# A two-layer hybrid mixer block: spare products redistributed around the triangular inverses, an ordering edge for the inverses' first matmuls, and the weights' low halves made in pieces of 256 columns

## The chip, the cores and the metric

The kernel runs on one core of one Trainium2 chip. The metric is the device time of one execution in microseconds (us). Three executions of the kernel before gave 1887.24, 1888.75 and 1889.05 us, so its median is 1888.75 us.

## The reference, cut to what matters

A block of depth 2 works on 512 tokens of width 1024 and on 256 context tokens. In each layer the normed and modulated activations `h` (and `hc` of the context) are projected by one wide matrix and split into three branches, their gates and three merge gates:

```python
parts = jnp.split(h @ w_in[layer], SPLIT_POINTS, axis=-1)
# a: gated delta rule, chunked, in both directions
lmat = jnp.where(strict, jnp.einsum('bhnid,bhnjd->bhnij', kb, k) * decay, 0.0)
tinv = lax.linalg.triangular_solve(lmat + eye, eye, left_side=True, lower=True)
# b: window attention with context keys; c: retention in both directions
merged = g_a * (y_a @ w_br[0]) + g_b * (y_b @ w_br[1]) + g_c * (y_c @ w_br[2])
x = x + gate * (merged @ w_o)
```

Branch a needs, per head, direction and chunk, the inverse of a unit triangular matrix. The gates of the three branches (`az`, `bz`, `cz`, four blocks of 128 columns each, through silu) and the merge gates (`m`, 24 blocks, through sigmoid) depend on `h` alone, not on what the branches compute. In layer 0 everything is also done for the context; in the last layer the context only needs what feeds keys and values.

## The kernel before, in words

Everything lies with channels on the partitions, 512 + 256 tokens along the free axis. A product with a block of 128 output columns (`proj`, line 317) splits the weights and the activations into a rounded high half and a low half: with eight blocks of 128 input channels it issues 16 matmuls with the high half of the weights (against `hh` and `hl`) and then 8 with the low half (`wl`, against `hh`), 24 of 512 columns into a PSUM bank of the pool `px` (two banks), and, where the context is wanted, 24 of 256 columns into the pool `pc` (one bank). `weight` (line 290) loads 512 KB by a DMA of the SP queue, makes the high half on ACT (line 278) and the low half on POOL by one subtraction of 128x1024 (line 287); `wr`, `wh` and `wl` have two buffers each. For the branch matrices of the merge there are four blocks of input channels, so half of all that.

**Spare products.** `aside` (line 1197) is a generator of 36 products a layer, in the order of `names`: az, bz, the first 8 of m, cz, and the other 16 of m. Each is read out of PSUM by ACT (tanh); an az, bz or cz also by one DVE instruction a bank (`stt`, line 281), which is the last reader of the bank. The result goes to DRAM by a DMA of the ACT queue and is loaded where it is needed. Since these products depend on `h` alone, the program mixes them into stages that are short of matmuls: `weave` interleaves generators, each with a number of steps, and `FILL` gives the number of spare products of each stage:

```python
weave((seq(self.delta_mats(l, last, st[0]), self.delta_inv(st[0])), 45),
      (self.delta_proj(l, 1, vec, last, st[1]), 6), fill(F[0]))
weave((self.hi(self.delta_chain(l, last, st[0])), 6), fill(F[1]))
weave((self.hi(self.delta_mats(l, last, st[1])), 4), fill(F[2]))
weave((self.hi(self.delta_inv(st[1])), 43), fill(F[3]))
weave((self.hi(self.delta_chain(l, last, st[1])), 6), fill(F[4]))
```

`F[5]` is the number after each of the attention's steps (12 in layer 0, 8 in layer 1) and `F[6]` the number before the token projection of branch c. What is left then is taken in the loop over `self.mods` and `self.fill` ahead of the merge. Before, layer 0 takes 20 in the five stages, 12 in the attention, 2 by `F[6]` and leaves 2; layer 1 takes 20, 8 and 2 and leaves 6.

**The inverses.** Heads go in two pairs, `st[0]` and `st[1]`. `delta_inv` (line 701) first inverts all 32x32 blocks on the diagonal at once by 31 steps of two DVE `tensor_tensor` each (lines 726 and 728, shown as line 284), each on the result of the last, with both inputs in SBUF. Then follow two transposes (731, 732) and 16 copies on DVE (747), with copies on ACT (749). `levels` (line 756) builds the 128x128 inverse from these by four bursts of small matmuls (line 774). A burst (line 262) chains its matmuls, so that they stand in one piece in TensorE's list, and makes the first of them wait for all that `made` names, the 16 DVE copies among it.

**What sets the order.** The framework writes each engine's list of instructions once, at compile time: at each moment of a modelled run it takes the ready instruction of the highest priority, where a place earlier in the program is a higher priority and `high_priority(offset)` raises it. On the chip each engine works through its list strictly in that order and waits at the head of it. The bursts, and in the second pair all of `delta_mats`, `delta_inv` and `delta_chain` (through `hi`), are raised by 3000; spare products and the projections have the plain priority and fill what is left. So a burst stands in TensorE's list at the place at which the modelled run had its inputs ready, with the spare products that weren't yet used up behind it.

After the second pair's chain come the normalisation of branch a, the attention, the token projection, the retention heads (`ret_head`), `c_norm` (line 936, ends in 16 to 24 `tensor_scalar` of line 954), the gates (`gated`, transposes of line 905), and the merge, whose first 8 products (branch a) don't depend on branch c.

Of the kernel before, what the change touches and what calls it, by code (L numbers as in the profile page):

```python
# [9 lines left out]
F32 = mybir.dt.float32  # L10
# [3 lines left out]
ALU = mybir.AluOpType  # L14
# [18 lines left out]
C1 = 3  # L33
AH = 2
BG = (0, 2)
FILL = ((2, 4, 2, 7, 5, 1, 2), (2, 3, 3, 7, 5, 1, 2))

NAMES = (["aq%d" % i for i in range(4)] + ["ak%d" % i for i in range(4)]
         + ["av%d" % i for i in range(4)] + ["az%d" % i for i in range(4)]
# [122 lines left out]
class Builder:  # L162
# [96 lines left out]
    def mm(self, out, lhsT, rhs, start=True, stop=True):  # L259
        return self.nc.tensor.matmul(out, lhsT=lhsT, rhs=rhs, start=start, stop=stop)  # L260

    def burst(self, todo, after):

        info = lambda c: mybir.DependencyInfo(c, mybir.DependencyReason.DATA)
        last = None
        with self.tc.high_priority(offset=HI):
            for f in todo:
                i = f().ins
                if last is None:
                    for a in after:  # L270
                        self.tc.add_manual_dep(i, a.ins.name, info(mybir.DependencyClass.Sync), reason="burst")
                else:
                    self.tc.add_manual_dep(i, last, info(mybir.DependencyClass.NoSync), reason="burst")
                last = i.name
# [15 lines left out]
    def weight(self, dram, kb=KB):  # L290
        nc = self.nc
        w = self.wr.tile([128, KB, 128], F32, name="wr")[:, 0:kb]
        hi = self.wh.tile([128, KB, 128], F32R, name="wh")[:, 0:kb]
        lo = self.wl.tile([128, KB, 128], F32R, name="wl")[:, 0:kb]
        with self.tc.high_priority(offset=WHI):
            nc.sync.dma_start(w, dram)
            self.act(hi, w, AF.Copy)
            self.gtt(lo, w, hi.bitcast(F32), ALU.subtract)
        return [hi[:, k] for k in range(kb)], [lo[:, k] for k in range(kb)]

    def prod(self, ps, w, acts, sl, ks=None):
        hi, lo = w
        n = len(acts)
        ks = ks or range(n)
        for k in ks:
            self.mm(ps, hi[k], acts[k][0].r[:, sl], start=(k == 0), stop=False)
            self.mm(ps, hi[k], acts[k][1].r[:, sl], start=False, stop=False)
        for k in ks:
            self.mm(ps, lo[k], acts[k][0].r[:, sl], start=False, stop=(k == n - 1))

    def proj(self, dram, acts, ctx, w=None):
        w = w or self.weight(dram, len(acts))
# [385 lines left out]
                self.free(df, db)  # L698
                yield

    def delta_inv(self, st):

        nc = self.nc
        Z, M, X = self.alloc_inv()
        nc.gpsimd.memset(Z, 0.0)
        nc.gpsimd.memset(X, 0.0)
        nc.gpsimd.memset(X[:, 0:1024:33], 1.0)
        blk = lambda s, q: s.f.rearrange("p (n c) -> p n c", c=128)[32 * q:32 * q + 32, :, 32 * q:32 * q + 32]  # L710
        sq = lambda t: t.rearrange("p (a b) -> p a b", b=32)
        lane = lambda t, q, d, hh: sq(t)[32 * q:32 * q + 32, :, d * 12 + hh * 6:d * 12 + hh * 6 + 6].rearrange(
            "p a n -> p n a")
        for hh, h in enumerate(st.heads):
            for q in range(4):
                self.act(lane(Z, q, 0, hh), blk(st.U[h], q), AF.Copy)
                nc.vector.transpose(out=lane(Z, q, 1, hh), in_=blk(st.U[h], q))
            yield
        nc.vector.transpose(out=M, in_=Z)
        yield  # L720
        mv, xv = sq(M), sq(X)
        ts = self.alloc()
        for m in range(31):
            n, w = 31 - m, m + 1
            tv = ts.f[:, 0:n * w].rearrange("p (r c) -> p r c", c=w)
            self.tt(tv, mv[:, m + 1:32, m:m + 1].to_broadcast([128, n, w]),
                    xv[:, m:m + 1, 0:w].to_broadcast([128, n, w]), ALU.mult)
            self.tt(xv[:, m + 1:32, 0:w], xv[:, m + 1:32, 0:w], tv, ALU.subtract)
            yield
        self.free(ts)  # L730
        nc.vector.transpose(out=Z, in_=X)
        nc.vector.transpose(out=sq(M), in_=xv.rearrange("p r c -> p c r"))
        yield
        W = st.W = {}
        T, Q = self.alloc(), self.alloc()
        nc.gpsimd.memset(Q.f, 0.0)
        six = lambda t: t.rearrange("p (h n c) -> p h n c", h=2, c=64)
        made = []
        for d in range(2):
            wsrc, tsrc = (Z, M) if d == 0 else (M, Z)  # L740

            own, other = (0, 2) if d == 0 else (3, 1)
            for hh, h in enumerate(st.heads):
                W[h, d] = self.alloc()
                nc.gpsimd.memset(W[h, d].f, 0.0)
                for q in range(4):
                    made.append(nc.vector.tensor_copy(blk(W[h, d], q), lane(wsrc, q, d, hh)))
                for q, t, c in ((own, Q, 32 * (own % 2)), (own + 1 - 2 * d, Q, 32 * (1 - own % 2)), (other, T, 0)):
                    made.append(self.act(six(t.f)[32 * q:32 * q + 32, hh, :, c:c + 32],
                                         lane(tsrc, q, d, hh), AF.Copy))  # L750
                yield
        self.free_inv()
        yield from self.levels(st, W, T, Q, made)
        self.free(T, Q, *st.U.values())

    def levels(self, st, W, T, Q, made):

# [8 lines left out]
        at = [(hh, h, ch) for hh, h in heads for ch in range(NCH)]  # L768
        sl = lambda a: slice(32 * a, 32 * a + 32)
# [3 lines left out]
        def mm(out, lhsT, rhs, pos):  # L773
# [2 lines left out]
        ps = bank(32)  # L776
        self.burst([mm(ps[sl(b), hh, ch], st.U[h].f[sl(a), ch * 128 + 32 * b:ch * 128 + 32 * b + 32],
                       t[sl(a), hh, ch, c:c + 32], (32 * a, 32 * b))
                    for hh, h, ch in at for a, b, d, t, c in pair], made)
        x = [self.act(xv[:, :, :, 0:32], ps, AF.Copy)]  # L780
        yield
        ps, pt = bank(32), bank(32)
# [414 lines left out]
    def aside(self, l, last):  # L1197
        nc = self.nc
        n = SEQ if last else TOK
        self.kept = {}  # L1200
        names = ["az%d" % i for i in range(4)] + ["bz%d" % i for i in range(4)]
        names += ["m%d_%d" % (r, d) for r in range(3) for d in range(8)]
        names[16:16] = ["cz%d" % i for i in range(4)]
        for nm in names:
            px, pc = self.pblk(l, nm, not last)
            t = self.fp.tile([128, TOK], F32, name="kept")
            for ps, sl in ((px, slice(0, SEQ)), (pc, slice(SEQ, TOK)))[:1 if last else 2]:
                self.act(t[:, sl], ps, AF.Tanh, scale=0.5)
# [15 lines left out]
    def layer(self, l, xs, rs, mod, vec, row, ada):  # L1224
# [9 lines left out]
        for k in range(KB):  # L1234
            self.tap("hh%d_%d" % (l, k), self.hs[k][0].f)
            self.tap("hl%d_%d" % (l, k), self.hs[k][1].f)
        self.fill = self.aside(l, last)
        self.mods = self.ada(ada) if ada else iter(())
        F = FILL[l]
# [37 lines left out]
        self.delta_gates(l, ba, row)  # L1277
        for _ in p0:
            pass
        weave((seq(self.delta_mats(l, last, st[0]), self.delta_inv(st[0])), 45),  # L1280
              (self.delta_proj(l, 1, vec, last, st[1]), 6), fill(F[0]))
        weave((self.hi(self.delta_chain(l, last, st[0])), 6), fill(F[1]))
        weave((self.hi(self.delta_mats(l, last, st[1])), 4), fill(F[2]))
        weave((self.hi(self.delta_inv(st[1])), 43), fill(F[3]))
        weave((self.hi(self.delta_chain(l, last, st[1])), 6), fill(F[4]))
        for t in st:
            oa.update(t.o)
# [154 lines left out]
def seq(*gens):  # L1442
    for g in gens:
        yield from g
# [34 lines left out]
```

## Time and profile before

| | |
|---|---|
| median of three executions | 1888.75 us |
| profiled execution | 1880.63 us |
| its span, first to last instruction | 1878.8 us |
| TensorE busy | 1721.2 us, 92% of the span |
| DVE, ACT, POOL busy | 1110.9, 844.3, 478.0 us |
| mean granted clock of TensorE | 0.968 of full speed |
| chain that ended last, by engine | PE 23%, DVE 7%, ACT 2% |

Where an engine is idle, the profile names the instruction whose end let it go on (its releaser). A line of the timeline merges like instructions that follow each other: start, time from first start to last end, engine, line, operation, output and inputs, count, and in brackets the idle time ahead of it with the releaser. The number behind a source line is that of the profile; helpers such as `mm` (260), `act` (278), `stt` (281), `tt` (284) and `gtt` (287) give their own line.

### The profile page before, as it was taken

To read this page: it belongs to the slowest core of one execution; us is meant where nothing else is said; L and a number is where in the kernel's file an instruction comes from. 1 tells how busy PE (TensorE), PEld (TensorE's weight loads), DVE (VectorE), ACT (ScalarE), POOL (GpSimd) and SP (SyncE) were. 2 spreads that over 40 slices of the span, in tenths; PEclk is the share of its full clock that TensorE was granted. 3 is DMA by queue.
4 is the path that set the end of the run, shared out by engine and by line. 5 is a ranking of instruction groups with operands and counts; after the bars stand their busy time and mean duration, and the time that the engine had idled before them with its cause. 6 is when DMAs were issued, how large, how long until landed. Compare 5 with 4: busy or idle time off the path is not lost. (4 is left out here: it accounts for less than half of the span.)

```text
span 1878.8 us, 30037 instructions
## 1 busy us (share of the span) xinstructions
PE 1721.2 (92%) x11574; PEld 1464.8 (78%) x11574; DVE 1110.9 (59%) x2531; ACT 844.3 (45%) x2018; POOL 478.0 (25%) x283
## 2 busy tenths in 40 slices
PE   7998799799899999999999899779698988999987
PEld 4887688698777779988888688668587766987876
DVE  4668948642663662355573648967856576253464
ACT  5564545442543553222223656456355465233234
POOL 1321402112212112122332513332213123123432
PEclk9999999899999999999999999889899999999998
DMA  8211112123234243115452111112223413114441
GB/s 309 69 35 42 65 30 92 64 94 120 83 108 155 85 135 112 43 51 169 130 176 96 63 41 67 51 62 68 94 76 119 140 62 113 34 57 160 152 153 68
DMA packets 73743, 180.63 MB, mean 96 GB/s; under 512 B 8832, under 2 KB 16384, under 8 KB 73600
## 3 DMA queue, kind: packets, MB, share of 16 engines
q1 hardware_dynamic: 62144, 154.07, 24.8%
q10 hardware_dynamic: 11456, 24.65, 3.4%
q8 instruction: 91, 1.49, 0.3%
q14 instruction: 52, 0.43, 0.1%
HBM read 150.89 MB, written 27.79 MB: 95 GB/s over the span
## 5 line engine op out<-in xcount | busy, mean ns | idle before, releaser
L287 POOL TENSOR_TENSOR wl<-wr,wh 128x1024 fp32r<-128x1024 f32 (+1 forms) x184 | 391.5, 2128 | 1215.7 <-ACT wh L278 811.6
L260 PE MATMUL px<-hh,wh 128*128 128x512 f32 (+1 forms) x1088 | 433.5, 402 | 22.8 <-DVE t L281 11.3
L260 PE MATMUL px<-hl,wh 128*128 128x512 f32 (+1 forms) x1088 | 432.2, 400 | 3.0 <-DVE hl L281 2.3
L284 DVE TENSOR_TENSOR t<-t,t 128x512 f32<-128x512 f32 (+21 forms) x411 | 299.0, 729 | 37.1 <-ACT t L278 25.6
L260 PE MATMUL px<-hh,wl 128*128 128x512 f32 (+1 forms) x1088 | 293.0, 400 | 0.0
L278 ACT ACTIVATE wh<-wr 128x1024 fp32r<-128x1024 f32 (+1 forms) x184 | 174.2, 947 | 213.8 <-PE pc L260 90.4
L260 PEld LDWEIGHTS px<-hh,wh 128*128 128x128 f32 x1088 | 209.6, 193 | 66.1 <-issue 10.7
L278 ACT ACTIVATE t<-t 32x192 f32<-32x192 f32 (+10 forms) x314 | 167.3, 545 | 207.0 <-DVE t L281 126.7
L260 PE MATMUL pg<-t,t 128*128 128x128 f32 (+2 forms) x1616 | 232.2, 287 | 21.0 <-DVE t L284 18.8
L260 PEld LDWEIGHTS px<-hl,wh 128*128 128x128 f32 x1088 | 210.1, 193 | 41.2 <-DVE hl L281 5.1
L260 PEld LDWEIGHTS pg<-t,t 128*128 128x128 f32 x1616 | 207.2, 192 | 43.7 <-issue 17.2
L260 PEld LDWEIGHTS px<-hh,wl 128*128 128x128 f32 x1088 | 202.6, 194 | 38.9 <-issue 2.0
L260 PE MATMUL pc<-hh,wh 128*128 128x256 f32 x696 | 177.6, 290 | 8.4 <-DVE t L281 7.8
L260 PE MATMUL pc<-hl,wh 128*128 128x256 f32 x696 | 179.0, 291 | 2.0 <-DVE hl L281 2.0
L260 PEld LDWEIGHTS pc<-hh,wh 128*128 128x128 f32 x696 | 134.8, 194 | 15.2 <-issue 7.1
L260 PEld LDWEIGHTS pc<-hl,wh 128*128 128x128 f32 x696 | 135.3, 194 | 7.3 <-DVE hl L281 3.2
L278 ACT ACTIVATE t<-pg 128x128 f32<-128x128 f32 (+4 forms) x216 | 77.6, 383 | 133.3 <-PE pg L403 37.1
L260 PE MATMUL pc<-hh,wl 128*128 128x256 f32 x696 | 103.7, 288 | 0.0
L278 ACT ACTIVATE t<-px 128x128 f32<-128x128 f32 (+2 forms) x120 | 54.4, 465 | 102.4 <-PE px L260 95.3
L260 PE MATMUL px<-t,wh 128*128 128x512 f32 x384 | 95.8, 392 | 0.1
L260 PEld LDWEIGHTS pc<-hh,wl 128*128 128x128 f32 x696 | 92.5, 195 | 0.8 <-issue 0.8
L260 PE MATMUL px<-t,hh 128*128 128x272 f32 (+1 forms) x384 | 88.3, 317 | 0.8 <-POOL t L287 0.6
(191 smaller groups left out, 2340.0 us busy)
## 6 DMA issues: line engine op xcount, KB each, us to landing
wr<-wblk SPq DMA_DIRECT2D x120, 512.0 KB, 3.2
t<-wada SPq DMA_DIRECT2D x48, 384.0 KB, 4.7
wr<-wbr SPq DMA_DIRECT2D x48, 256.0 KB, 2.7
m<-kept ACTq DMA_DIRECT2D x24, 384.0 KB, 2.3
t<-m SPq DMA_DIRECT2D x24, 384.0 KB, 3.7
wr<-wout SPq DMA_DIRECT2D x16, 512.0 KB, 3.2
t<-wada SPq DMA_DIRECT2D x24, 256.0 KB, 4.8
m<-kept ACTq DMA_DIRECT2D x24, 256.0 KB, 2.1
```

The source lines that it names most:

```text
L260: return self.nc.tensor.matmul(out, lhsT=lhsT, rhs=rhs, start=start, stop=stop)
L278: return self.nc.scalar.activation(out, in_, func, **k)
L284: self.nc.vector.tensor_tensor(out=out, in0=in0, in1=in1, op=op)
L287: self.nc.gpsimd.tensor_tensor(out=out, in0=in0, in1=in1, op=op)
```

## The change

Four things. (1) `FILL` takes 5 and 6 instead of 2 spare products beside the first pair's inverse, in layer 1 also 9 instead of 7 beside the second pair's; layer 0 takes one less ahead of the token projection. The five stages now take 23 and 26, and nothing is left for the loop ahead of the merge. (2) The order of the 36 is m (6), az, m (2), bz, m (4), cz, m (12). (3) The first matmul of the first burst (those of 32x32) is ordered behind the last matmul of the spare product that was issued as the second last (third last for the second pair of layer 0) when `levels` begins; this is an order in TensorE's list, no semaphore. (4) The low half of the weights is made by a subtraction for each two of the 128-column blocks: four of 128x256 instead of one of 128x1024, two instead of one of 128x512.

```diff
-FILL = ((2, 4, 2, 7, 5, 1, 2), (2, 3, 3, 7, 5, 1, 2))
+FILL = ((5, 4, 2, 7, 5, 1, 1), (6, 3, 3, 9, 5, 1, 2))
+BACK = ((2, 3), (2, 2))
...
-    def burst(self, todo, after):
+    def burst(self, todo, after, behind=None):
...
                     for a in after:
                         self.tc.add_manual_dep(i, a.ins.name, info(mybir.DependencyClass.Sync), reason="burst")
+                    if behind:
+                        self.tc.add_manual_dep(i, behind, info(mybir.DependencyClass.NoSync), reason="behind")
...
-            self.gtt(lo, w, hi.bitcast(F32), ALU.subtract)
+            for k in range(0, kb, 2):
+                self.gtt(lo[:, k:k + 2], w[:, k:k + 2], hi[:, k:k + 2].bitcast(F32), ALU.subtract)
...
-            self.mm(ps, lo[k], acts[k][0].r[:, sl], start=False, stop=(k == n - 1))
+            self.last = self.mm(ps, lo[k], acts[k][0].r[:, sl], start=False, stop=(k == n - 1)).ins.name
...
-        yield from self.levels(st, W, T, Q, made)
+        yield from self.levels(st, W, T, Q, made, self.asides[-back])
...
-                    for hh, h, ch in at for a, b, d, t, c in pair], made)
+                    for hh, h, ch in at for a, b, d, t, c in pair], made, behind)
...
-        names = ["az%d" % i for i in range(4)] + ["bz%d" % i for i in range(4)]
-        names += ["m%d_%d" % (r, d) for r in range(3) for d in range(8)]
-        names[16:16] = ["cz%d" % i for i in range(4)]
-        for nm in names:
+        z = lambda b: ["%sz%d" % (b, i) for i in range(4)]
+        ms = ["m%d_%d" % (r, d) for r in range(3) for d in range(8)]
+        for nm in ms[0:6] + z("a") + ms[6:8] + z("b") + ms[8:12] + z("c") + ms[12:]:
             px, pc = self.pblk(l, nm, not last)
+            self.asides.append(self.last)
```

## Rows read from the trace of the kernel before

**Rows 1.** Who waited for whom on TensorE: total us, times, longest us.

```profile
PE pg L774 <- DVE t L747: 39.7, 4, 16.5
PE px L260 <- DVE t L281: 11.6, 4, 6.4
```

**Rows 2.** Stretches: length, busy us (instructions) by engine, clock, DMA share, GB/s.

```profile
144.00:234.00 90.00, 73.80 (x411) 62.31 (x409) 83.66 (x183) 44.37 (x106) 26.29 (x18) 0.96 0.16 56
...
338.00:362.00 24.00, 11.62 (x362) 10.54 (x361) 15.16 (x40) 11.18 (x24) 0.00 (x0) 0.72 0.17 57
1150.00:1244.00 94.00, 73.53 (x364) 61.19 (x362) 88.39 (x180) 48.45 (x112) 30.51 (x19) 0.92 0.19 65
...
1340.00:1369.00 29.00, 11.71 (x351) 9.47 (x350) 19.57 (x51) 10.88 (x24) 2.35 (x1) 0.71 0.20 65
...
1724.00:1800.00 76.00, 76.00 (x336) 62.99 (x336) 34.25 (x40) 22.43 (x37) 34.17 (x24) 1.00 0.51 161
```

**Rows 3.** TensorE's timeline around the first bursts of the four inverses, and by c_norm.

```profile
234.23 1.50 PE L774 MATMUL pg<-t,t 32*32 32x32 f32 x96 [6.00 <-DVE t L747]
236.26 1.91 PE L260 MATMUL px<-hh,wl 128*128 128x512 f32 x4
...
338.36 0.28 PE L260 MATMUL pc<-hl,wh 128*128 128x256 f32 x1
350.39 1.51 PE L774 MATMUL pg<-t,t 32*32 32x32 f32 x96 [11.76 <-DVE t L747]
...
1238.37 0.61 PE L260 MATMUL px<-hh,wl 128*128 128x512 f32 x2
...
1244.38 1.50 PE L774 MATMUL pg<-t,t 32*32 32x32 f32 x96 [5.40 <-DVE t L747]
...
1339.56 1.52 PE L260 MATMUL px<-hh,wl 128*128 128x512 f32 x6
1357.58 1.50 PE L774 MATMUL pg<-t,t 32*32 32x32 f32 x96 [16.50 <-DVE t L747]
...
1716.39 0.33 PE L905 MATMUL pg<-c,t 128*128 128x128 f32 x1 [2.17 <-DVE t L954]
```

**Rows 4.** ACT's timeline: reading out spare products.

```profile
324.45 0.36 ACT L278 ACTIVATE kept<-pc 128x256 f32<-128x256 f32 x1
...
332.79 0.37 ACT L278 ACTIVATE kept<-pc 128x256 f32<-128x256 f32 x1
...
1234.94 0.60 ACT L278 ACTIVATE kept<-px 128x512 f32<-128x512 f32 x1 [0.75 <-PE px L260]
...
1330.69 0.60 ACT L278 ACTIVATE kept<-px 128x512 f32<-128x512 f32 x1 [0.70 <-PE px L260]
...
1336.13 0.60 ACT L278 ACTIVATE kept<-px 128x512 f32<-128x512 f32 x1 [0.70 <-PE px L260]
```

**Rows 5.** The tile `kept`: its DVE instructions, ns min/median/max, first and last start.

```profile
L281 DVE SCALAR_TENSOR_TENSOR kept<-kept,px x24: 670/680/690, 138.7 to 1419.2; 128x512 f32<-128x512 f32 x24
```

**Rows 6.** DVE's timeline in the second inverse of layer 1.

```profile
1315.59 34.08 DVE L284 TENSOR_TENSOR t<-t,t 128x31 f32<-128x31 f32 x62
...
1352.65 4.79 DVE L747 COPY t<-t 32x192 f32<-32x192 f32 x16
```

**Rows 7.** DVE by shape between 1333 and 1340 us.

```profile
L284 DVE TENSOR_TENSOR t<-t,t 128x247 f32<-128x247 f32 x1 | 2.5, 2495 | 0.0
L284 DVE TENSOR_TENSOR t<-t,t 128x252 f32<-128x252 f32 x4 | 1.7, 421 | 0.1
```

**Rows 8.** POOL's timeline between 1312 and 1360 us, last of five such rows.

```profile
1336.23 2.39 POOL L287 TENSOR_TENSOR wl<-wr,wh 128x1024 fp32r<-128x1024 f32 x1 [2.95 <-PE px L260]
```

**Rows 9.** POOL's subtractions by shape over the span: count, busy us, mean ns.

```profile
L287 POOL TENSOR_TENSOR wl<-wr,wh 128x1024 fp32r<-128x1024 f32 x136 | 328.2, 2413 | 1097.5 <-ACT wh L278 717.0 <-PE px L260 198.7 <-PE pc L260 89.7
L287 POOL TENSOR_TENSOR wl<-wr,wh 128x512 fp32r<-128x512 f32 x48 | 63.3, 1319 | 118.1 <-ACT wh L278 94.6 <-PE px L260 22.6 <-PE pc L260 1.0
...
L287 POOL TENSOR_TENSOR t<-t,t 128x272 fp32r<-128x272 f32 x16 | 13.9, 891 | 6.5 <-ACT t L278 5.7 <-issue 0.4 <-DVE t L284 0.4
```

More of the change, by code (lines that the diff above doesn't have):

```diff
@@ L699, in delta_mats, with delta_inv @@
                 yield
-    def delta_inv(self, st):
+    def delta_inv(self, st, back):
         nc = self.nc
@@ L752, in delta_inv, with levels @@
         self.free_inv()
-        yield from self.levels(st, W, T, Q, made)
+        yield from self.levels(st, W, T, Q, made, self.asides[-back])
         self.free(T, Q, *st.U.values())
-    def levels(self, st, W, T, Q, made):
+    def levels(self, st, W, T, Q, made, behind):
         nc = self.nc
@@ L1236, in layer @@
             self.tap("hl%d_%d" % (l, k), self.hs[k][1].f)
+        self.asides = []
         self.fill = self.aside(l, last)
@@ L1279, in layer @@
             pass
-        weave((seq(self.delta_mats(l, last, st[0]), self.delta_inv(st[0])), 45),
+        weave((seq(self.delta_mats(l, last, st[0]), self.delta_inv(st[0], BACK[l][0])), 45),
               (self.delta_proj(l, 1, vec, last, st[1]), 6), fill(F[0]))
@@ L1283, in layer @@
         weave((self.hi(self.delta_mats(l, last, st[1])), 4), fill(F[2]))
-        weave((self.hi(self.delta_inv(st[1])), 43), fill(F[3]))
+        weave((self.hi(self.delta_inv(st[1], BACK[l][1])), 43), fill(F[3]))
         weave((self.hi(self.delta_chain(l, last, st[1])), 6), fill(F[4]))
```

## The prediction

> **What bounds the kernel now.** I read the page first: TensorE is busy for 92% of the span, so nearly every stage is held by matmuls, and a change that adds none can win only idle time and time at the lower clock. Then the list of waits of TensorE. The longest entry by far is the 32x32 bursts' wait for DVE's copies, four times, 39.7 us [rows 1]. The table of stretches shows where: TensorE idles for 16.2 us (90.0 less 73.8) beside layer 0's first inverse, 12.4 us around its second, 20.5 and 17.3 us in layer 1, 66 us together, and these stretches have a granted clock of 0.71 to 0.96; behind them the merge is solid, 76 us of 76 at 1.00 [rows 2]. So a spare product moved from the end of a layer into such a hole saves its whole length. The table says too that beside the first inverses DVE is the bound (83.7 us of 90, 88.4 of 94).
>
> **How long a spare product is.** Products read out one behind the other are 8.34 us apart in layer 0 and 5.44 us in layer 1 [rows 4]; the difference, 2.9 us, is the context's 24 matmuls, and 512 columns cost 5.44/24 = 0.227 us each.
>
> **Where the bursts stand now.** Counting the read-outs of ACT from the layer's start, rows 4 end with the tenth product of layer 0 and the fourteenth of layer 1 ahead of the second inverses' bursts. Layer 0's first burst stands in the fourth product with eight low-half matmuls and the context's part still behind it; layer 1's in the fifth, six low-half matmuls behind it; layer 0's second in the eleventh (place 10.7), layer 1's in the fifteenth, 22 of 24 done (14.9) [rows 3]. The change puts them behind products 4, 5, 16 and 20 (of 5, 6, 18 and 21 issued by then).
>
> **Part 1, the first inverses.** The extra three and four products change little here: the list already reaches the fourth and the fifth. What moves ahead of the burst is 8 x 0.227 + 2.9 = 4.7 us in layer 0, into a wait of 6.0, and 6 x 0.227 = 1.4 us in layer 1, into one of 5.4 [rows 3]. The new order helps DVE: gates of branch a, with 0.68 us a bank on DVE [rows 5], stood beside the inverse, and merge blocks, with none, take their place. That is two px banks and one smaller one in layer 0 (I take 1.8 us), two in layer 1 (1.4), one to one in the span, since DVE is the bound. Sum: 6.5 and 2.8 us.
>
> **Part 2, the second inverse of layer 0.** 5.3 more products of 8.34 us, 44 us, come ahead of the burst; the hole of 11.76 us [rows 3] is covered, and TensorE comes to the burst about 28 us later than now, which costs nothing as long as products are left for the chain behind it: 23 are issued by the end of that stage, so 7 remain against 9.3 now. What is late next is a bank of PSUM: products 13 to 16 are now branch b's gates, whose DVE read-out must stand behind the 16 copies in DVE's list (the modelled run had the copies done at place 10.7 to 11.3). The 14th can't fill `pc` until the 13th's is read; TensorE, at place 11.3 at 338.4, gets there 0.7 x 8.34 + 8.34 + 5.44 us later, at 358. DVE's copies now end as the burst begins, at 350.4, and two or three more subtractions of POOL (part 4: 2.4 to 3.6 us each) fall among them: 355 to 361. I take 3 us of wait, between 0 and 5. The clock around this burst is 0.72 of full [rows 2]; the 256-column matmuls behind the burst run at half rate for some 4.6 us, so 2.3 us come back. Sum: 11.8 - 3 + 2.3 = 11 us.
>
> **Part 3, the second inverse of layer 1.** Here I expect little, for the same reason. DVE's run takes 34.1 us and the copies end at 1357.4 [rows 6]. Five subtractions of POOL lie in it. A two-input instruction that meets one takes 2.50 us where its neighbour takes 0.42 [rows 7], just as long as POOL's 2.39 [rows 8]; so 12 of the 34 us are waits for POOL, which the compile-time order doesn't foresee: DVE falls 10 us and more behind the list. Products 13 to 16 are branch b's gates here too, and only two px banks exist; TensorE is known to wait for a bank that DVE still holds (11.6 us in four waits) [rows 1]. By the modelled places the 13th's read-out stands in the last steps of DVE's run, so the 15th product can't start before about 1350, while TensorE is ready for it at 1336.1 - 1.4 = 1334.7: a hole of 15.5 us instead of 16.5. Behind it products 15 to 20 run without a hole, 33 us, and the burst comes near 1383. Sum: 1 us; the ends are a gain of 16.5 and a loss of 5.
>
> **Part 4, the pieces.** A subtraction of 1024 columns takes 2.413 us, one of 512 1.319: 2.14 ns a column and 0.225 us each [rows 9]. One of 256 is then 0.77 us; the nearest row, 272 columns, gives 0.89. Four take 3.1 to 3.6 us instead of 2.4. For POOL (478 us of 1879) this is hidden, and products wait for no `wl`. What counts is how long DVE is shut out: in the run, where every instruction has two inputs in SBUF, between 0 and 1.15 us more for each half; where instructions that read PSUM stand between them, up to 0.5 us less, because DVE can pass after each piece; in the attention a blocked instruction loses at most a piece instead of 2.4 us. I put 0 in the inverses and a gain of 2 us (0 to 6) in the attention.
>
> The Trainium skill (SBUF — State Buffer, "Who interferes with whom") says that the shared port pair is locked for a whole instruction by whoever starts first, and that the other fully blocks. Rows 7 and 8 agree with it. By that rule alone, with POOL always first, four locks would cost DVE 3.1 us instead of 2.4; that is the fourth case below.
>
> **Part 5, the ends of the layers.** Two products fewer in layer 0 and six fewer in layer 1 stand beside c_norm. TensorE already waits 2.17 us there [rows 3] with products to spare. Merge products of branch a (half of 24 matmuls, 2.7 us, eight of them) can take their place, but each needs a DVE read-out behind c_norm's instructions. I charge 2 us in layer 1 and 1 in layer 0; the bounds are 0 and the 16 us that two products in layer 0, or three in layer 1, now cover.
>
> **Sum.** 6.5 + 2.8 + 11 + 1 + 2 - 3 = 20.3 us off the profiled execution's 1880.63 us, 1.1%. That execution lies 8.1 us, 0.4%, below the median; the saving is in waits of fixed length, so I take it off the median: 1888.75 - 20.3 = 1868.5.
>
> **Rivals.**
> *The gates don't hold TensorE* (25%). If the read-outs of products 13 to 16 stand earlier in DVE's list, TensorE runs on to the burst behind product 20, near 1368, and five or six more subtractions push DVE to 1370 to 1377. The burst moves by 16 us while 27 us more work is done: 11 us more, and 3 more in layer 0. 1854. For it: read-outs slip between the run's steps in layer 0 now. Against it: the places above.
> *The ends are laid bare* (10%). If merge products don't fill the time beside c_norm, 16 us come back in layer 1 and some in layer 0: 1886, about no change. Against it: eight products are independent of branch c, and ACT and POOL have room (22 and 34 us of 76 in the merge) [rows 2].
> *The change doesn't bite*: for the first pair this is nearly my forecast; for the second it can't be, since the order is forced.
> *The pieces make DVE later* (12%), the case on the other side. Place: the inverses' steps, where DVE is the bound. There are 15 subtractions beside the first inverses and 7 in the second of layer 1. At 0.89 us a piece, all shut out, each costs 1.15 us: 25 us against 20.3, so slower by 5, 1894. It decides from 0.92 us a subtraction. The rule quoted above, with 0.77, would give 15 us and leave 5 of gain, 1884.
>
> **How the numbers follow.** The forecast has 45%, with a range of its own from 1861 to 1878; the gates free 25%, the bare ends 10%, the pieces 12% (of it half below no change by the smaller price), the rest 8% spread. A measurement can tell 0.2%, 3.8 us, from no change. Faster by more: 45 + 25 + a third of 10 + half of 12 + a part of the rest, 0.81. Within: 0.08. Slower: the other half of 12, a third of 10 and a part of the rest, 0.11. The range takes in the free gates and the bare ends: 1851 to 1886.
>
> **What would show it.** Right: the burst of layer 0 that waits 11.76 us now finds its copies done; TensorE's largest hole in layer 1 ends with a matmul into px released by DVE's line 281, not with a burst; the burst follows the 20th product at once; POOL's rows show 256 columns at 0.77 to 0.9 us and no DVE step of 2.5 us. Wrong: a burst of layer 1 that still waits over 5 us for line 747; DVE's run longer than 36 us; idle time of over 5 us ahead of line 905 in layer 1, or among the first merge products.

## The result, and the profile after

The changed kernel takes 1827.82 us (median of 4 runs, 1825.61 to 1832.75) against 1887.99 us (1886.0 to 1889.05) before: a ratio of 0.9686 with a 95% interval from 0.9668 to 0.9704, 60 us faster. The forecast was 1868.5 with a range from 1851 to 1886: right in its sign, a third of the size, and the result lies outside the range.

The profiled execution of after has a span of 1831.0 us (1878.8 before); TensorE is busy for 1722.7 us of it (94%), so its idle time fell from 157.6 to 108.3 us, by a little more than the 47.8 us between the spans. The profiled execution of before (1880.63 us) is faster than its other runs, and that of after (1832.75 us) is the slowest of its four, so the profiles lie 48 us apart and the medians 60. VectorE's busy time fell by 54 us, from 1110.9 to 1057.2, with the same 2531 instructions. TensorE's waits in after (who waited for whom, total us, times, longest; the 10.9 us of the first row are the wait for the first data, at the start of the kernel):

```profile
PE pg L261 <- DVE t L288: 24.3, 16, 10.9
...
PE px L261 <- DVE kept L285: 12.2, 5, 4.7
...
PE pc L261 <- DVE kept L285: 5.3, 1, 5.3
...
PE pg L779 <- DVE t L752: 2.9, 2, 1.8
```

Line 752 is line 747 of before: the bursts' wait of 39.7 us [rows 1] is down to 2.9. New are the waits for `kept`, 17.5 us: TensorE waits for a PSUM bank that a gate's read-out holds (before had 0.8 us of them). TensorE's timeline of after, the four first bursts and the holes ahead of the last (start, us, [idle before <- releaser]):

```profile
245.57 1.12 PE L779 MATMUL pg<-t,t 32*32 32x32 f32 x96 [1.77 <-DVE t L752]
...
382.66 1.02 PE L779 MATMUL pg<-t,t 32*32 32x32 f32 x96
...
1217.57 1.50 PE L779 MATMUL pg<-t,t 32*32 32x32 f32 x96 [1.13 <-DVE t L752]
...
1306.47 0.50 PE L261 MATMUL px<-hh,wh 128*128 128x512 f32 x1 [3.42 <-DVE kept L285]
...
1321.06 0.50 PE L261 MATMUL px<-hh,wh 128*128 128x512 f32 x1 [1.78 <-DVE kept L285]
...
1331.45 0.58 PE L261 MATMUL px<-hh,wh 128*128 128x512 f32 x1 [4.66 <-DVE kept L285]
...
1349.62 1.02 PE L779 MATMUL pg<-t,t 32*32 32x32 f32 x96
```

The four waits of 6.00, 11.76, 5.40 and 16.50 us [rows 3] have become 1.77, none, 1.13 and none, with three holes of 9.9 us in place of the last (a fourth of 2.13 us lies further ahead, at 1280.99).

Another part came from where the number of spare products stayed as it was. The attention stage of layer 0 and of layer 1 by the table of stretches, first before (length, busy us and instructions of TensorE, weight loads, VectorE, ScalarE and GpSimd, then the clock, the DMA share and GB/s):

```profile
490.20:703.90 213.70, 204.20 (x1421) 162.19 (x1421) 118.74 (x358) 102.95 (x300) 35.23 (x18) 0.98 0.35 118
...
1445.00:1588.80 143.80, 131.73 (x819) 98.35 (x819) 96.09 (x252) 78.35 (x226) 31.52 (x16) 0.98 0.31 101
```

and after:

```profile
499.50:703.50 204.00, 199.47 (x1416) 158.22 (x1417) 112.61 (x360) 102.75 (x300) 44.46 (x57) 1.00 0.37 126
...
1438.00:1572.20 134.20, 129.58 (x818) 96.34 (x820) 88.72 (x252) 78.47 (x226) 40.79 (x51) 1.00 0.34 113
```

The same instructions, but for a few at the edges, take 9.7 and 9.6 us less: TensorE idles less (9.5 to 4.5 us, 12.1 to 4.6), and the granted clock went from 0.98 to 1.00. With the pieces alone (`e1` below) the same two stages show nearly as much:

```profile
485.20:690.00 204.80, 200.45 (x1421) 158.80 (x1421) 112.42 (x358) 102.89 (x300) 44.67 (x57) 1.00 0.38 125
...
1412.90:1548.50 135.60, 130.93 (x819) 97.26 (x819) 88.41 (x252) 78.31 (x226) 40.62 (x51) 0.99 0.34 112
```

One place of layer 0's attention in before shows what was lost there (timelines of GpSimd, VectorE and TensorE):

```profile
554.28 0.48 DVE L1117 TENSOR_SCALAR t<-t,bred 128x512 f32<-128x512 f32 x1
...
555.12 2.36 POOL L287 TENSOR_TENSOR wl<-wr,wh 128x1024 fp32r<-128x1024 f32 x1 [17.81 <-ACT wh L278]
...
555.27 2.50 DVE L1117 TENSOR_SCALAR t<-t,bred 128x512 f32<-128x512 f32 x1
...
557.82 0.55 PE L1125 MATMUL pg<-c,t 128*128 128x128 f32 x3 [1.42 <-DVE t L1117]
```

The softmax's normalisation, 0.48 us long, takes 2.50 when it begins 0.15 us after a subtraction of 2.36; it ends 0.3 us after it, and TensorE's transposes wait for it. The same place in after:

```profile
560.73 3.17 POOL L291 TENSOR_TENSOR wl<-wr,wh 128x256 fp32r<-128x256 f32 x4 [16.33 <-ACT wh L282]
...
560.88 0.87 DVE L1122 TENSOR_SCALAR t<-t,bred 128x512 f32<-128x512 f32 x1
561.67 0.68 DVE L285 SCALAR_TENSOR_TENSOR bred<-bred,ns 128x1 f32<-128x1 f32 x1
...
562.66 0.66 DVE L1122 TENSOR_SCALAR t<-t,bred 128x512 f32<-128x512 f32 x1
```

Four pieces take 3.17 us together, and VectorE gets its turn between them: it waits for a piece, not for the weight.

### The profile page after: what moved, and what is told of

The parts are those of the page before. It is cut to its first block, busy times and chain, and to the rows that moved or that the text cites. A ratio compares the mean times of both kernels' runs of the same rounds, so it can differ in the third digit from the quotient of the medians.

```text
span 1831.0 us, 30644 instructions
## 1 busy us (share of the span) xinstructions
PE 1722.7 (94%) x11574; PEld 1463.0 (80%) x11574; DVE 1057.2 (58%) x2531; ACT 844.7 (46%) x2018; POOL 591.5 (32%) x739
## 5 line engine op out<-in xcount | busy, mean ns | idle before, releaser
L291 POOL TENSOR_TENSOR wl<-wr,wh 128x256 fp32r<-128x256 f32 x640 | 503.8, 816 | 1056.5 <-ACT wh L282 797.2
L261 PE MATMUL px<-hh,wl 128*128 128x512 f32 (+1 forms) x1088 | 286.7, 393 | 0.0
L288 DVE TENSOR_TENSOR t<-t,t 128x512 f32<-128x512 f32 (+21 forms) x411 | 252.4, 616 | 40.1 <-ACT t L282 27.3
L261 PE MATMUL pg<-t,t 128*128 128x128 f32 (+2 forms) x1616 | 231.2, 285 | 11.3 <-DVE t L288 10.9
L261 PEld LDWEIGHTS pg<-t,t 128*128 128x128 f32 x1616 | 206.0, 191 | 34.1 <-issue 11.6
L261 PEld LDWEIGHTS px<-hh,wl 128*128 128x128 f32 x1088 | 198.6, 191 | 38.0 <-issue 2.0
L261 PE MATMUL px<-t,wh 128*128 128x512 f32 x384 | 100.3, 397 | 4.8 <-DVE t L285 4.6
```

The costliest lines, as they stand in the source:

```text
L288: self.nc.vector.tensor_tensor(out=out, in0=in0, in1=in1, op=op)
L291: self.nc.gpsimd.tensor_tensor(out=out, in0=in0, in1=in1, op=op)
```

## The experiments

Eighteen kernels, each beside runs of the kernel before on the same chip. The medians of before lay between 1886.2 and 1888.6 us, so each run is compared by what it saves against its own before, and differences of 2 us are not told apart.

| run | median us (range) | ratio, 95% | saves |
|---|---|---|---|
| after | 1827.82 (1825.61 to 1832.75) | 0.9668 to 0.9704 | 60.2 |
| e1_pieces_only | 1835.32 (1833.25 to 1836.52) | 0.9701 to 0.9742 | 51.5 |
| e2_no_pieces | 1881.82 (1874.21 to 1886.47) | 0.9954 to 0.9989 | 5.0 |
| e3_gates_later | 1831.01 (1826.59 to 1833.69) | 0.9667 to 0.9724 | 55.8 |
| e4_no_edge | 1832.47 (1829.92 to 1835.79) | 0.9686 to 0.9731 | 54.3 |
| e5_pieces_512 | 1851.48 (1845.42 to 1851.74) | 0.9784 to 0.9827 | 36.1 |
| e6_pieces_128 | 1811.04 (1804.53 to 1812.94) | 0.9562 to 0.9613 | 76.5 |
| e7_pieces_backwards | 1830.06 (1827.44 to 1831.56) | 0.9681 to 0.9716 | 57.5 |
| e8_whole_in_attention | 1850.57 (1846.08 to 1850.88) | 0.9784 to 0.9822 | 37.0 |
| e9_layer0_products_only | 1829.40 (1826.27 to 1832.41) | 0.9672 to 0.9714 | 57.9 |
| e10_layer1_products_only | 1837.14 (1835.46 to 1841.84) | 0.9716 to 0.9760 | 50.2 |
| e11_pieces_64 | 1817.05 (1814.23 to 1821.48) | 0.9607 to 0.9652 | 70.3 |
| e12_before_pieces_128 | 1825.87 (1824.51 to 1826.91) | 0.9654 to 0.9695 | 61.5 |
| e13_gate_copy | 1830.21 (1828.23 to 1832.09) | 0.9683 to 0.9712 | 56.7 |
| e14_64_in_inverses | 1800.87 (1797.41 to 1801.94) | 0.9525 to 0.9553 | 86.0 |
| e15_128_layer0_only | 1814.50 (1813.24 to 1817.68) | 0.9602 to 0.9634 | 72.4 |
| e16_three_banks | 1814.04 (1810.88 to 1816.06) | 0.9593 to 0.9632 | 72.2 |
| e17_three_banks_64 | 1788.89 (1786.35 to 1790.11) | 0.9465 to 0.9496 | 97.4 |
| e18_before_banks_256 | 1833.78 (1832.44 to 1835.06) | 0.9691 to 0.9723 | 54.8 |

**Which half of the change pays.** The pieces alone, in the kernel before:

```
-            self.gtt(lo, w, hi.bitcast(F32), ALU.subtract)
+            for k in range(0, kb, 2):
+                self.gtt(lo[:, k:k + 2], w[:, k:k + 2], hi[:, k:k + 2].bitcast(F32), ALU.subtract)
```

> The kernel before with the low halves in pieces of 256 columns and nothing else; TensorE's list is that of the kernel before. Theory P (the pieces give what the forecast missed: DVE was busy 53.7 us less after the change, and the forecast gave the pieces 2 us): 20 to 30 us faster than before, 1858 to 1868, most of it beside the first inverses and in the attention; DVE busy near 1060; the waits of the second inverses' bursts stay at 9 to 17 us. Theory F (the products and their order give nearly all): 0 to 5 us faster, 1883 to 1888.

and the same two lines undone in the kernel after:

> The changed kernel with the low halves made by one subtraction as before; TensorE's list is that of the changed kernel. Theory P: about half of the gain is left, 1853 to 1863, DVE busy again near 1110 and single steps of the inverses' run at 2.5 us. Theory F: 1828 to 1833. If the two parts add up, the savings of this run and of the pieces alone make the 60 us of the whole change.

The pieces alone save 51.5 us, the products and their order 5.0, both 60.2. Both runs lie far outside the ranges of theory P, which gave the pieces about half of the gain; they have nearly all of it. Two rows of TensorE's waits in before (10.9 us of the first are again the start of the kernel, which the next list puts down to a DMA):

```profile
PE pg L260 <- DVE t L284: 32.7, 15, 10.9
PE pg L595 <- DVE t L281: 15.7, 9, 3.5
```

with the pieces alone:

```profile
PE pg L775 <- DVE t L748: 40.1, 4, 14.8
PE pg L260 <- DVE t L284: 13.8, 15, 1.8
...
PE pg L596 <- DVE t L281: 6.2, 4, 2.1
```

and with the products alone (11.1 us of the first row are the start):

```profile
PE pg L261 <- DVE t L288: 34.5, 15, 11.1
PE pg L599 <- DVE t L285: 24.6, 11, 3.7
...
PE px L261 <- DVE kept L285: 12.8, 6, 4.6
...
PE pc L261 <- DVE kept L285: 6.7, 1, 6.7
...
PE pg L778 <- DVE t L751: 4.4, 2, 2.6
```

With the pieces alone the bursts still wait 40 us and the kernel is 51.5 us faster; with the products alone that wait is gone and almost nothing is gained. The longest wait of the profile was not where the time lay.

**What in the pieces pays.** Two ways: VectorE gets in between them (S), or TensorE's low products start sooner (H). The size of a piece, with `kb` cut in steps of 4, 1 and half a block:

> The kernel after with the low halves in pieces of 512 columns (two of about 1.32 us a weight). Theory S (an instruction of DVE with two operands in SBUF waits for the end of the POOL piece that runs): the mean wait that an arriving instruction meets grows with the sum of the squares of the pieces, 2.41^2 = 5.8 for the whole, 2 x 1.32^2 = 3.5 for halves, 4 x 0.75^2 = 2.25 for quarters; so halves give back (5.8 - 3.5) / (5.8 - 2.25) = 65% of the 54 us between 1881.8 (whole) and 1827.8 (quarters): 1845 to 1850. Rival A (one gap in each subtraction is enough): 1828 to 1834. Rival H (the gain is that the first low blocks are ready sooner): near S, so it isn't told apart here.

> The kernel after with the low halves in pieces of 128 columns (eight a weight). Theory S: by the squares, if a piece of 128 takes 0.45 to 0.6 us, 8 x 0.45^2 = 1.6 to 8 x 0.6^2 = 2.9, so between 10 us faster and 10 us slower than quarters: 1818 to 1838, with POOL busy for more of each weight. Rival B (every cut helps by as much again): below 1810. Rival C (POOL becomes late with the low halves, since a weight's eight pieces take 3.6 to 4.8 us): TensorE then waits for wl, over 1840.

> The kernel after with the low halves in pieces of 64 columns (sixteen a weight). A piece took 2.41, 1.33, 0.74 and 0.46 us at 1024, 512, 256 and 128 columns, so an estimate for 64 is 0.3 to 0.35 us, 4.8 to 5.6 us a weight. Theory S (the squares of the pieces: 16 x 0.33^2 = 1.7 against 8 x 0.46^2 = 1.7): no gain over 128 columns, 1806 to 1816. Rival B (each halving gives as much as the last, 17 us): 1792 to 1798. Rival C (POOL is late with the low halves): TensorE waits for wl, over 1818.

GpSimd's subtractions by shape (count, busy us, mean ns) in after and with pieces of 128 and of 64:

```profile
L291 POOL TENSOR_TENSOR wl<-wr,wh 128x256 fp32r<-128x256 f32 x640 | 503.8, 816 | 1056.5 <-ACT wh L282 797.2 <-ACT t L282 177.1 <-issue 42.4
```

```profile
L291 POOL TENSOR_TENSOR wl<-wr,wh 128x128 fp32r<-128x128 f32 x1280 | 621.3, 520 | 937.3 <-ACT wh L282 704.3 <-ACT t L282 161.7 <-issue 37.3
```

```profile
L291 POOL TENSOR_TENSOR wl<-wr,wh 128x64 fp32r<-128x64 f32 x2560 | 836.0, 364 | 754.0 <-ACT wh L282 547.2 <-ACT t L282 141.8 <-issue 38.6
```

Halves took 1851.5, 1.5 us above what S gave for them; 128 columns took 1811.0, 7 us below its range and just short of rival B's. So the size matters in the way of S, but its rule of squares gives the amounts only roughly. With 64 VectorE is freer still (busy for 1005 us against 1027), but the kernel is 6 us slower, one us past S's upper end: sixteen pieces of 364 ns are 5.8 us of GpSimd a weight. The stretch around the layer boundary and the last products are each some 6 us longer than with 128, and TensorE's waits for what GpSimd makes are 4.5 us instead of 2.3. The opposite order of the four pieces:

```
-            for k in range(0, kb, 2):
+            for k in reversed(range(0, kb, 2)):
```

> The kernel after with the four pieces of a weight made in the opposite order, so that the two blocks that TensorE multiplies first are ready last, when all four are done. Theory S (only the gaps between pieces count): 1825 to 1833, no change. Rival H (TensorE begins the low products at the first piece, 2.1 us before the last): the gain goes, and the time is at that of the single subtraction, 1875 to 1885.

No change that can be told: H, which gave 1875 to 1885, falls. Then the place, with single subtractions in the attention alone:

```
+            c = kb if self.whole else 2
...
+        self.whole = True
         yb = [self.ysplit(t, n) for t in self.branch_b(l, row, vb, last)]
+        self.whole = False
```

> The kernel after with single subtractions for the weights that are asked for inside the attention stage of each layer alone (about 24 of 184), pieces of 256 everywhere else. Theory S with the loss where DVE is on the chain (DVE's normalisation, maxima and rotations between TensorE's products): the attention stages lost 11.5 and 13 us to single subtractions in the traces, so 1848 to 1854. Rival (every weight costs its share, 54 / 184 = 0.29 us): 1834 to 1836.

30 weights fell under it, and they cost 23.2 us (60.2 less 37.0): 0.77 us each, against 0.21 for the other 154 (the remaining 32.0 of the 55.2 us that all single subtractions cost). A subtraction is dearest in the attention, where VectorE stands between two of TensorE's products, and not where VectorE is busy longest. With H gone, this and the sizes leave S.

**Why the products give so little.** The gates later in the order of the spare products, so that the second inverses have merge blocks, which VectorE doesn't read:

```
-        for nm in ms[0:6] + z("a") + ms[6:8] + z("b") + ms[8:12] + z("c") + ms[12:]:
+        for nm in ms[0:6] + z("a") + ms[6:16] + z("b") + z("c") + ms[16:]:
```

> The changed kernel with ten merge blocks between branch a's gates and branch b's, so that the products ahead of the second inverses' bursts are read out by ACT alone. Theory of the held banks (the forecast's part 3: a gate's read-out stands late in DVE's list and keeps a PSUM bank): TensorE's waits for DVE's instructions on kept, 12.2 and 5.3 us, nearly vanish and the kernel is 8 to 16 us faster than the changed one, 1812 to 1820. Rival (the bursts then wait for the copies instead, since DVE is late in any case): the waits move to the first matmul of the burst and the time is within 4 us of 1828.

Without the edge that puts the 32x32 products behind the spare ones (the dependency on `behind` left out):

> The changed kernel without the ordering edge. TensorE's list then has the second pairs' bursts 155 matmuls earlier in layer 0 and 88 earlier in layer 1, the first pairs' where they are. Theory E (the edge covers the second bursts' waits): they wait 8 to 17 us again for the copies, 10 to 25 us slower than the changed kernel, 1838 to 1853. Rival (TensorE idles there anyway, at a gate's bank or at the burst): within 5 us of 1828.

Neither gains: they save 4.4 and 5.9 us less than after, so the edge is worth some 6 us at most and the order of the gates does not free TensorE. Without the edge the second bursts do wait again, 9.83 us in layer 0 and 6.84 in layer 1, much as theory E said, but the time grows by less than it gave. With the gates later the wait for `kept` is there still, but now for ScalarE's read-out:

```profile
PE px L261 <- ACT kept L282: 9.4, 2, 8.7
...
PE pc L261 <- ACT kept L282: 4.8, 1, 4.8
```

So that run didn't free the banks: ScalarE's queue, too, holds steps of the inverse that wait for VectorE, and a merge block's read-out stands behind them. The layers apart, FILL and BACK of one layer at a time as in after (the order of the 36 stays that of after in both layers):

> The kernel after with layer 1's spare products and order of the second inverse as before, so that the new products and order are those of layer 0 alone; pieces of 256 kept. Theory L (read from the two traces with pieces, with and without the new products: layer 0 ends 5 us sooner with them, layer 1 no sooner, since there TensorE holds two more products behind the end of DVE's run in the second inverse): 1826 to 1832. Rival (both layers carry half of the 7.5 us): 1831 to 1834.

> The kernel after with layer 0's spare products and order as before, so that the new products and order are those of layer 1 alone; pieces of 256 kept. Theory L: 1833 to 1837, that is the time of pieces alone (1835.3). Rival (layer 1's waits of 8.7 and 14.8 us at the first 32x32 products, which pieces alone leave, are what the products fill): 1812 to 1825.

Layer 0's products are worth 6.4 us (57.9 less 51.5), layer 1's nothing (50.2 less 51.5). With 128 columns (the second again with the order of after in both layers):

> The kernel before with the low halves in pieces of 128 columns and nothing else changed. If pieces and products add up (at 256 columns the products gave 7.5 us): 1815 to 1822. Rival (with DVE freer the products fill more of the waits at the first 32x32 products): 1823 to 1830. Rival (the products are worth nothing once DVE is free): 1808 to 1813.

> Pieces of 128 columns with layer 0's new products and order, and layer 1's as before. Theory L (layer 1's products are worth nothing, as in the run with layer 0 alone at 256 columns, 1829.4 against 1827.8): 1809 to 1814, the time of the run with pieces of 128 and all products (1811.0). Rival (with VectorE's run shorter the products of layer 1 carry half of the 14.8 us that they give in all at 128 columns): 1816 to 1820.

All products are worth 15.0 us there (76.5 less 61.5), layer 1's 4.1 of them, between the two expectations: so the products give more where VectorE is freer. Then the bank itself. First ScalarE copies a gate's bank out, and VectorE multiplies from the copy:

```
-                    self.stt(t[:, sl], t[:, sl], 1.0, ps, ALU.add, ALU.mult)
+                    k = sl.stop - sl.start
+                    u = self.fp.tile([128, k], F32, name="raw%d" % k, bufs=1)
+                    self.act(u, ps, AF.Copy)
+                    self.stt(t[:, sl], t[:, sl], 1.0, u, ALU.add, ALU.mult)
```

> The kernel after with one edit to the gates' read-out: ScalarE copies the PSUM bank into SBUF (0.58 us more of ScalarE for each of the 12 gate products) and VectorE multiplies from the copy, so that the bank is free without VectorE. Theory B (TensorE's waits for kept on VectorE, 12.2 + 5.3 us in the kernel after, are banks held by VectorE's read-outs behind its run in the inverses, and cost their length): those waits fall to under 5 us and the time to 1812 to 1820. Rival R (the stage is as long as VectorE's run, and what TensorE gains on one wait it loses on the next): 1824 to 1833, with another releaser in the place of kept.

```profile
PE px L261 <- ACT raw L282: 12.1, 3, 9.1
...
PE pc L261 <- ACT raw L282: 7.1, 1, 7.1
```

The wait moved once more, whole, to the copy. Ahead of the wait of 9.1 us VectorE had read the copy before by 1318.4, so its one buffer was free; ScalarE's list held the next read-out back, behind its own 12 copies of the inverse, which wait for VectorE's transposes (ScalarE's timeline):

```profile
1321.41 5.78 ACT L282 ACTIVATE t<-t 32x192 f32<-32x192 f32 x12 [1.49 <-DVE t L736]
1327.21 0.60 ACT L282 ACTIVATE kept<-px 128x512 f32<-128x512 f32 x1
1327.71 0.59 ACT L282 ACTIVATE raw<-px 128x512 f32<-128x512 f32 x1
```

The same stands in after ahead of its hole of 4.66 us, where the profile names VectorE alone:

```profile
1306.44 0.33 ACTq L1217 DMA_DIRECT2D bz<-kept  x1
1306.89 1.06 ACT L282 ACTIVATE wh<-wr 128x1024 fp32r<-128x1024 f32 x1 [8.65 <-DVE t L288]
...
1323.15 5.96 ACT L282 ACTIVATE t<-t 32x192 f32<-32x192 f32 x12 [7.58 <-DVE t L736]
...
1330.10 0.58 ACT L282 ACTIVATE kept<-px 128x512 f32<-128x512 f32 x1
```

The first two of these rows show one thing more: the DMA that stores a gate is in ScalarE's list too. It comes 0.03 us after the end of VectorE's product (1306.41), and the weight's high half and the next read-out come behind it. So a bank is held by ScalarE's list as well as by VectorE's run, and this run doesn't decide. Three banks for the 512-column products do:

```
-        self.px = pool(name="px", bufs=2, space=PSUM)
+        self.px = pool(name="px", bufs=3, space=PSUM)
...
-        self.pg = pool(name="pg", bufs=5, space=PSUM)
+        self.pg = pool(name="pg", bufs=4, space=PSUM)
```

> The kernel after with three PSUM banks for the 512-column products instead of two, and four for the small products instead of five. Theory B (banks held behind the run are what the products wait for): TensorE's waits of px for kept (12.2 us) fall to under 4 us, and the time by 5 to 12 us, to 1816 to 1823, unless the small products miss their bank. Rival R (the stage is as long as VectorE's run, and the products are only moved about in it): 1825 to 1832. Rival P (the small products need their five banks): over 1835, with waits of pg that the kernel after doesn't have.

> The kernel before with pieces of 256 columns and three PSUM banks for the 512-column products, four for the small ones; its spare products and order are those of before. Theory B (the banks let the new products fill the waits): the banks alone give little here, 1830 to 1836, so the products are worth 16 to 22 us with them, which is what the prediction gave them. Rival D (the banks serve every product, those of before too): 1818 to 1825, and the products are worth 4 to 11 us as with two banks.

```profile
PE px L261 <- ACT wh L282: 8.4, 4, 6.1
PE pc L261 <- DVE kept L285: 6.7, 2, 6.5
```

With a third bank `px` no longer waits for `kept` (what is left is the one `pc` bank), and the kernel takes 1814.0, 2 us below the range of theory B. New is the first row, the wait for a weight's high half: 6.1 us of it stand in layer 1's second inverse, behind the same 12 copies of ScalarE. The last first burst comes without a wait, at 1335.69 instead of 1349.62:

```profile
1335.69 1.02 PE L779 MATMUL pg<-t,t 32*32 32x32 f32 x96
```

In the kernel before with pieces the same banks bring 3.3 us (54.8 less 51.5). So with room for them the products and their order are worth 17.4 us (72.2 less 54.8) against 8.7 with two banks (60.2 less 51.5): the banks held them back. Where, is shown by the lengths of four stretches in the profiled executions (one each, in us), cut at the first transpose of the retention heads in either layer (line 1039 of after) and at the first of the delta rule's projection in layer 1 (line 600). The change moves two products, 16.7 us, in layer 0 and six, 32.6 us, in layer 1 from behind the cut at the heads to ahead of it:

| stretch | pieces alone | after | three banks, products of before | three banks, products of after |
|---|---|---|---|---|
| start to layer 0's heads, 2 products more in after | 762.6 | 767.9 | 754.6 | 760.5 |
| to layer 1, 2 fewer | 303.4 | 293.1 | 307.8 | 291.8 |
| to layer 1's heads, 6 more | 530.2 | 559.1 | 531.3 | 554.2 |
| to the end, 6 fewer | 237.3 | 210.9 | 239.6 | 206.5 |

Ahead of the heads the holes take 11.4 us in layer 0 (16.7 less 5.3) and 3.7 in layer 1 (32.6 less 28.9); with three banks 10.8 and 9.7. Behind them, the products' leaving gives back only 10.3 of 16.7 us in layer 0 and 26.4 of 32.6 in layer 1; with three banks all but 0.7. So the third bank pays in layer 1's holes and at the ends of the layers. Six profiled executions with two banks, pieces of 256 and as many spare products in layer 0 as after have 292.9 to 293.9 us for its end, so that loss is clear; for layer 1's end six have 206.0 to 210.9 us, 208 in the mean, so its loss is nearer to 3 us than to 6.

**A version that beats both.** Pieces of 64 columns for the weights that are asked for in the delta rule's matrices and inverses, where VectorE is the bound, and 128 elsewhere; then the same with three banks:

```
+        self.cut = 64
         weave((seq(self.delta_mats(l, last, st[0]), self.delta_inv(st[0], BACK[l][0])), 45),
...
+        self.cut = 128
         weave((self.hi(self.delta_chain(l, last, st[1])), 6), fill(F[4]))
...
+            c = self.cut
+            for k in range(0, kb * 128, c):
+                b = slice(k % 128, k % 128 + c)
+                self.gtt(lo[:, k // 128, b], w[:, k // 128, b], hi[:, k // 128, b].bitcast(F32), ALU.subtract)
```

> The kernel after with pieces of 64 columns for the weights that are asked for in the delta rule's matrices and inverses (four stretches, two a layer), and of 128 everywhere else. Theory S by stage (in the traces 64 columns everywhere took 7 us off layer 0's inverses and 3 to 5 off layer 1's against 128, and lost 5 at the layer boundary and 6 at the last products, where POOL takes 5.8 us a weight and VectorE isn't the bound): 1799 to 1806. Rival (what the inverses gain is given back later, or POOL is late in them as well): 1808 to 1816.

> The kernel with pieces of 64 columns in the inverses and 128 elsewhere (1800.9), with the same banks. Theory B: 1790 to 1797. Rival R: 1798 to 1804. Rival P: over 1808.

The first takes 1800.9 us, within S's range; the second 1788.9, a microsecond below theory B's, 5.2% faster than before and 2.1% faster than after.

## Why the prediction failed

**Part 4, the pieces: the step that failed.** It gave 0 us in the inverses and 2 (0 to 6) in the attention; the pieces gave 51.5, and that puts the result outside the range. Its reason was the right one, "a blocked instruction loses at most a piece instead of 2.4 us", and its price was wrong in two ways. In the two attention stages, where a blocked normalisation or rotation is what TensorE waits for, it put 2 us where single subtractions cost some 23. And the other stages were put at nothing or not priced. TensorE's list is the same in before and with the pieces alone, so the same matmul can be found in both profiled executions, which are 45 us apart: 17 us of this come in the two attention stages, 11 in the stages of the four inverses (6 of it in layer 1's first, with its matrices and projections), 7 in the chains behind the second ones and 11 from the retention heads to the end of either layer. The trace of before had the row: the normalisation's 80 instructions reach from 352 to 2576 ns around a median of 490. VectorE's 79 two-input instructions of 512 columns show it over the span (count, busy us, mean ns), before and after:

```profile
L284 DVE TENSOR_TENSOR t<-t,t 128x512 f32<-128x512 f32 x79 | 81.5, 1034 | 5.5 <-ACT t L278 4.2
```

```profile
L288 DVE TENSOR_TENSOR t<-t,t 128x512 f32<-128x512 f32 x79 | 63.1, 801 | 7.0 <-ACT t L282 5.6
```

In the inverse's run, where every instruction has two inputs, Part 4 was nearly right: layer 1's second run of 62 instructions, 34.08 us before [rows 6], takes 31.99 with the pieces alone, 2.1 us less for five subtractions (what else the inverses' stages gave is not in this run):

```profile
1288.95 31.99 DVE L284 TENSOR_TENSOR t<-t,t 128x31 f32<-128x31 f32 x62
```

The price of a piece was right too: 0.77 us was worked out for 256 columns, 816 ns were measured in the mean.

**The rival on the other side** (the pieces make VectorE later, 12%) needed VectorE to wait for all four pieces. It doesn't: the normalisation that takes 0.48 us alone takes 0.87 beside four pieces of 3.17, and VectorE's busy time fell. By the Trainium skill (SBUF — State Buffer, "Who interferes with whom") the engine that comes second is blocked for the whole instruction of the first. The normalisation above agrees at either size: it takes 2.50 us beside an instruction of 2.36, and 0.87 beside pieces of 0.8. What the rival added, that GpSimd is always first again, no row of after shows.

**Parts 1 to 3 and 5, the products.** They gave 6.5 + 2.8 + 11 + 1 - 3 = 18.3 us; measured were 5.0 with whole subtractions and 8.7 with pieces. The waits went where the parts said, and the holes came where they said, as waits for `kept`: Part 3 charged one of 15.5 us in layer 1's second inverse, and after has four of 12.0 there; Part 2 charged 3 in layer 0's, and it has 5.25. But the sum didn't follow. By the table of four stretches, Parts 1 and 2 gave layer 0's holes 17.5 us, and they took 11.4; for layer 1 Parts 1 and 3 gave 3.8, and 3.7 were measured. Part 5 charged 1 us for layer 0's end, and it cost 6.4; the 2 us for layer 1's end were about right (3 in the mean). Of the 6.4, 2.5 us are idle time of TensorE, 1.9 of it a wait for VectorE's read-out in the merge's `pc`; the rest is that the matmuls follow each other less closely. The same at both layers' ends makes up some 8 of the 11 us by which the same 11574 matmuls take more of TensorE's time in after (1722.7) than with the pieces alone (1711.5). Why they do so is not shown; with three banks they take 1713.4. That the products' 17.4 us with a third bank come near the forecast of 18.3 is luck: the forecast had already taken off 3 and 15.5 us for held banks, and would have been 36.8 without them. One reading was off too: Part 2's 2.3 us for the clock rest on 4.6 us of 256-column matmuls at half rate behind the burst, and the trace of before has five of them there, 1.4 us, between small matmuls.

The rival of the bare ends, with about no change as its time, falls; that of free gates (1854) falls too, since its gates did hold banks.

## What to carry to other kernels

An engine that is busy for a quarter of the time can set the pace of one on the critical path: look for one form of instruction that at times takes some five times its median, find the other engine's instruction that ends with it, and price it by who waits there, in every stage, not only where the blocked engine is busiest. Cutting the blocker into pieces is cheap to try; the best size depends on the stage, small where the blocked engine is the bound and larger where the blocker is late itself. And a hole that independent work is to fill needs somewhere to put the results, and an engine whose list lets it take them out: a long wait that vanishes from the list without the time falling has moved, and one more bank tells whether that is why. Count the work's absence at its old place as well: it can cost there what it gains in the hole.

## What the runs showed of the hardware

- GpSimd's 32-bit subtraction took 2413, 1346, 816, 520 and 364 ns for 1024, 512, 256, 128 and 64 columns on 128 partitions, in the mean over one profiled execution each: within 6% of 0.22 us and 2.14 ns a column at every size. So a piece of 64 is still some 60% fixed cost, and worth it in the inverses, where VectorE is the bound.
- After the holes of 3.42 and 4.66 us in layer 1's second inverse the 512-column matmuls of after start 0.43 us apart for some 3 us instead of 0.227, which is the lower of TensorE's two levels (1.2 GHz); after the first of them that begins with the seventh matmul, after the second at once. The granted clock of the two 12-us stretches from 1302 and from 1326, with these holes, is 0.86, and 1.00 in the one between, whose hole is of 1.78 us. In the timeline, after the second of them and then back at the full rate:

```profile
1332.68 0.63 PE L261 MATMUL px<-hl,wh 128*128 128x512 f32 x1
1333.11 0.63 PE L261 MATMUL px<-hh,wh 128*128 128x512 f32 x1
...
1336.13 0.39 PE L261 MATMUL px<-hl,wh 128*128 128x512 f32 x1
1336.36 0.40 PE L261 MATMUL px<-hh,wh 128*128 128x512 f32 x1
```
